# A hybrid backbone on one core: the gate matmuls of the recurrence branch interleaved with the next projection in another ratio, the last round filled with the first tile of the branch's gate projection, and its weights loaded one tile ahead

## The chip, the cores and the metric

One core of one Trainium2 chip. The metric is the device time of one execution in microseconds (us). Before the change three runs gave 1374.14, 1374.28 and 1376.15 us (median 1374.28).

## The reference

The program is a two-layer backbone over 1024 latent tokens of width 1024, with 256 context tokens. Layer 0 has two branches side by side. Branch A is a gated convolution (31 taps along the sequence, layer norm, SiLU). Branch B, which the change touches, is a gated linear recurrence in both directions:

```python
z = h @ p["w_in"]
va, vg, ga, xb, gb = jnp.split(z, [W_CONV, 2 * W_CONV, 3 * W_CONV, 3 * W_CONV + W_LRU], axis=-1)
y_a = conformer_conv(va, vg, p) * jax.nn.silu(ga)
y_b, hT = rglru_branch(xb, p, h0, True)
y_b = y_b * jax.nn.silu(gb)
return jnp.concatenate([y_a, y_b], axis=-1) @ p["w_out"], hT
```

In `rglru_branch` `xb` goes through a short convolution (4 taps) to `u`; two small matrices for each head and direction give the gates r and i (sigmoids); then a = exp(-8 r softplus(-lam)), the input is sqrt(1 - a^2) i u, and h = a h + input is scanned forwards and backwards, first over the context, then over the latent tokens. Layer 1 is a pooling mixer with two large projections; a final norm ends the program.

## The kernel before

Channels lie on the 128 partitions, tokens along the free dimension; the 1024 channels are 8 tiles (`KT` = 8). Every fp32 product is split into three matmuls of rounded parts: hi x hi, hi x lo, lo x hi (`mm3_steps`, L126 to L128, one step for each of the 8 tiles that are summed). A weight tile comes by DMA to `wr_*`, ScalarE (ACT) casts the high part `wh_*` (L95), GpSimd (POOL) subtracts for the low part `wl_*` (L96). `wr`, `wh` and `wl` have two buffers each (`wpool`), so a weight's cast waits until the matmuls of the weight before the last one are done. Results of 512 columns go to PSUM banks of the pool `pm` (4 of them, used in turn); `wide` tiles of 1024 columns lie in `pc`.

The branches of layer 0 start in a loop of 8 rounds, one for each channel tile j:

- the short convolution makes `uc` from the projections `xbc` (256 context columns) and `xb` (1024 latent columns): one ACT row (L531) and three VectorE (DVE) rows (L534) each; `uh` and `ul` (L538, L571) are its two parts.
- `decays(j - 1)` works on ACT: tanh of the r gates of the round before, their exp, and the root (all L449).
- `vg` and `va` are projected (48 matmuls each); ACT takes sigmoid(vg) as `sg` (L552), behind the root; DVE multiplies to `u` (L564), which also frees `va`'s two PSUM banks.
- `recurrence(j - 1)`: POOL multiplies (L463, L465), DVE forms the input (L468) and scans each direction over 256 (L475) and over 1024 (L477) columns; the sum of both (L480) is stored to DRAM (`yb_raw`).
- the gates of round j: 12 banks, of 256, 512 and 512 columns for each of the four gate tiles, three matmuls each (L508 to L510), ACT's sigmoid behind each (L511). Their steps are written interleaved with the 24 steps of the next round's `xb` projection (8 for the context, 16 for the latent columns), two after each bank, by `weave`.

In the last round there is no next `xb`: the `va` steps are interleaved with the gates instead. Behind the loop, the gate projection `gb` of branch B is made tile by tile (ACT's SiLU L726, DVE's product L727), then its output projection `wob`, while DVE works on the 31 taps of branch A's convolution (L746, 240 rows of about 1000 columns), which it takes up wherever it has nothing more urgent, from the first round on.

The written order isn't the order of issue. A scheduler orders the rows of each engine by priority and by its own estimate of when their inputs are ready; the order is fixed when the program is built, and each engine then works its queue in that order. `issue_after` and `high_priority` bind or move single rows. So a change in the written order moves rows on all engines.

Of the kernel before, what the change touches and what calls it, by code (L numbers as in the profile page):

```python
# [11 lines left out]
AF = mybir.ActivationFunctionType  # L12
# [3 lines left out]
P = 128  # L16
# [4 lines left out]
KT = D // P  # L21
# [34 lines left out]
def body(ctx, tc, xT, ctxT, cc, ccol, modT, modW, win, gw, wout, wu, grp, wg, wo1, small, edge, ident, outT):  # L56
# [30 lines left out]
    def psum(name):  # L87
        return pm.tile([P, H], F32, tag="mm", name=name)
# [341 lines left out]
    with ExitStack() as actx:  # L430
# [83 lines left out]

        def weave(some, others, n):
            for _ in some:
                for _ in range(n):
                    next(others, None)
            for _ in others:
                pass  # L520

        state = None
# [3 lines left out]
        for j in range(KT):  # L526
# [38 lines left out]

            gws = wload(gw[j], f"gw{j}", nc.gpsimd, n=4 * P) if last else None
            with ExitStack() as octx:
                if not last:
                    weave((), value_steps(), 1)
                    octx.enter_context(tc.issue_after(taken[0].ins))  # L570
                nc.vector.tensor_tensor(out=ul, in0=uc, in1=uh.bitcast(F32), op=sub)  # L571
            if last:
                weave(gate_steps(j, gws, (uh, ul), gates), value_steps(), 1)
            if j == 0:
# [4 lines left out]
            if state is not None:  # L579
                recurrence(j - 1, *state, roots)  # L580
            if not last:
                xb, steps = project_xb(j + 1)
                gws = wload(gw[j], f"gw{j}", nc.gpsimd, n=4 * P)
                weave(gate_steps(j, gws, (uh, ul), gates), steps, 2)
            state = uc, gates
        recurrence(KT - 1, *state, decays(KT - 1, state[1])[0])

# [127 lines left out]

    bh, bl = [], []
    for j in range(KT):
        w = wload(win[4 * KT + j], f"gb{j}", nc.gpsimd)
        th, tl = d2tile(f"ybh{j}", F32R), d2tile(f"ybl{j}", F32R)
        for h in range(2):  # L720
            ps = psum(f"gb{j}_{h}")
            mm3(ps, w, (hh, hl), HALF[h])
            y = vtile(f"yr{j}_{h}")
            nc.sync.dma_start(y, yb_raw[j][:, HALF[h]])
            sgt = ttile(f"sb{j}_{h}")
            nc.scalar.activation(sgt, ps, AF.Silu)  # L726
            nc.vector.tensor_tensor(out=y, in0=y, in1=sgt, op=mult)  # L727
            split(y, th[:, HALF[h]], tl[:, HALF[h]], nc.gpsimd)
        bh.append(th)
        bl.append(tl)  # L730
# [701 lines left out]
```

## Time and profile before

| | |
|---|---|
| median of 3 runs | 1374.28 us |
| profiled execution | 1381.07 us, its span 1379.3 us |
| PE (matmul) busy | 1295.9 us, 94% of the span |
| DVE busy | 1205.1 us, 87% |
| ACT busy | 632.7 us, 46% |
| POOL busy | 363.3 us, 26% |
| granted TensorE clock, mean | 0.974 |

The rounds lie between about 93 and 476 us of the span, `gb` up to 570, `wob` up to about 672. In rows of the profile a line is engine, line of the program, operation, output and inputs; "idle before" names what ended the engine's wait. A row of a timeline gives start and duration in us; consecutive rows overlap by a little, so what a row costs its engine is read from start to start.

### The profile page before, as it was taken

Reading aid. Unit: us, or ns where it says so; the run is one execution under the profiler, and the core shown is the slowest. Engines: PE = TensorE matmul, PEld = TensorE weight load, DVE = VectorE, ACT = ScalarE, POOL = GpSimd, SP = SyncE. Lnnn points to the kernel's source line nnn. Section 1 sums busy time; section 2 is a strip of 40 time slices with the busy share of each in tenths; the row PEclk is TensorE's granted clock in tenths of the full one; section 3 lists DMA queues with packets and bytes.
Section 4 is the critical chain, followed back from the end, with each engine's and each line's share of the span. In section 5 each row is a group of like instructions: output and inputs, shape, how many; then the busy total and the mean of one; then the engine's idle time right before and its main releaser. Section 6 shows DMA issues by size and latency. Waiting matters only on the chain.

```text
span 1379.3 us, 15637 instructions
## 1 busy us (share of the span) xinstructions
PE 1295.9 (94%) x5664; PEld 1048.2 (76%) x5664; DVE 1205.1 (87%) x1587; ACT 632.7 (46%) x906; POOL 363.3 (26%) x182
## 2 busy tenths in 40 slices
PE   7889989898999799999998999999999999999896
PEld 4468868787777587787887887788888888778685
DVE  7998999999999999998778865999999987876775
ACT  6353644674465542304533544754334344634442
POOL 5173534743473555523320004000000000000002
PEclk9899999999999899999999999999999999999997
DMA  9753011111112113343353646424243334758623
GB/s 354 280 180 119 25 59 54 53 40 61 54 35 72 46 46 130 110 151 135 103 185 122 221 154 205 138 93 151 100 145 123 115 115 132 265 190 275 206 107 123
DMA packets 82866, 181.79 MB, mean 132 GB/s; under 512 B 7778, under 2 KB 27618, under 8 KB 82788
## 3 DMA queue, kind: packets, MB, share of 16 engines
q1 hardware_dynamic: 74340, 176.60, 37.8%
q10 hardware_dynamic: 8448, 4.20, 1.0%
q8 instruction: 44, 0.72, 0.2%
q14 instruction: 34, 0.28, 0.1%
HBM read 136.72 MB, written 44.04 MB: 131 GB/s over the span
## 4 chain that ended last, share of the span: by engine, by line
PE 36%; DVE 10%; DMA 7%; issue 2%; ACT 2%; POOL 1%; POOLq 0%; SPq 0%; DVEq 0%; ACTq 0%
PE ga L127 2%; PE ga L128 2%; PE ga L126 2%; PE wob L127 2%; PE wob L128 2%; PE wob L126 2%; DMA wr_g<-wg 1%; DVE ws L986 1%; DMA yr_t<-y_t 1%; DMA wr_v<-wfold 1%; PE qb_g L666 1%; DVE wq_g L96 1%; PE qb_g L669 1%; PE qb_g L668 1%; DVE wq_wo L96 1%
## 5 line engine op out<-in xcount | busy, mean ns | idle before, releaser
L746 DVE SCALAR_TENSOR_TENSOR conv<-u,sm,conv 128x1013 f32<-128x1013 f32 (+14 forms) x232 | 291.2, 1272 | 6.6 <-ACT conv L738 3.8
L1252 POOL TENSOR_TENSOR o<-x,rr 128x256 f32<-128x256 f32 (+1 forms) x9 | 8.0, 923 | 462.9 <-ACT rr L1240 460.0
L511 ACT ACTIVATE g<-g,sm 128x512 f32<-128x512 f32 (+1 forms) x96 | 58.8, 617 | 110.5 <-PE g L510 108.3
L96 POOL TENSOR_TENSOR wl_wu<-wr_wu,wh_wu 128x1024 fp32r<-128x1024 f32 x16 | 39.4, 2470 | 153.9 <-ACT wh_wu L95 147.7
L463 POOL TENSOR_TENSOR g<-g,uc 128x1280 f32<-128x1280 f32 x16 | 47.5, 2967 | 107.9 <-ACT g L511 65.1
L249 PE MATMUL fold<-gh,wh_wu 128*128 128x512 f32 x128 | 53.0, 416 | 5.7 <-ACT wh_wu L95 5.7
L250 PE MATMUL fold<-gl,wh_wu 128*128 128x512 f32 x128 | 52.4, 409 | 3.2 <-DVE gl L96 3.2
L128 PE MATMUL gb<-h0h,wl_gb 128*128 128x512 f32 x128 | 50.7, 398 | 4.8 <-POOL wl_gb L96 4.8
L126 PE MATMUL vg<-h0h,wh_vg 128*128 128x512 f32 x128 | 52.3, 408 | 2.7 <-ACT g L511 2.1
L251 PE MATMUL fold<-gh,wl_wu 128*128 128x512 f32 x128 | 50.7, 405 | 2.3 <-POOL wl_wu L96 2.3
L128 PE MATMUL xb<-h0h,wl_xb 128*128 128x512 f32 x128 | 50.2, 392 | 2.0 <-POOL wl_xb L96 2.0
L127 PE MATMUL wob<-ybl,wh_wob 128*128 128x512 f32 x128 | 50.5, 395 | 1.2 <-POOL ybl L96 1.2
L465 POOL TENSOR_TENSOR g<-g,th 128x1280 f32<-128x1280 f32 x16 | 46.9, 2948 | 16.8 <-ACT th L449 16.8
L127 PE MATMUL vg<-h0l,wh_vg 128*128 128x512 f32 x128 | 51.2, 400 | 0.0
L126 PE MATMUL gb<-h0h,wh_gb 128*128 128x512 f32 x128 | 50.6, 395 | 0.1
L126 PE MATMUL va<-h0h,wh_va 128*128 128x512 f32 x128 | 50.6, 395 | 0.0
L127 PE MATMUL va<-h0l,wh_va 128*128 128x512 f32 x128 | 50.6, 395 | 0.0
L508 PE MATMUL g<-uh,wh_gw 128*128 128x512 f32 (+1 forms) x96 | 36.3, 379 | 15.1 <-ACT wh_gw L95 6.4
L126 PE MATMUL wob<-ybh,wh_wob 128*128 128x512 f32 x128 | 50.6, 396 | 0.0
L128 PE MATMUL wob<-ybh,wl_wob 128*128 128x512 f32 x128 | 49.9, 391 | 0.7 <-POOL wl_wob L96 0.7
L128 PE MATMUL va<-h0h,wl_va 128*128 128x512 f32 x128 | 50.4, 395 | 0.0
L127 PE MATMUL gb<-h0l,wh_gb 128*128 128x512 f32 x128 | 50.4, 393 | 0.0
(548 smaller groups left out, 4301.1 us busy)
## 6 DMA issues: line engine op xcount, KB each, us to landing
mod<-modT SPq DMA_DIRECT2D x28, 512.0 KB, 5.5
wr_wu<-wu SPq DMA_DIRECT2D x16, 512.0 KB, 3.9
x_part<-xp SPq DMA_DIRECT2D x32, 256.0 KB, 2.4
mod<-modT SPq DMA_DIRECT2D x32, 256.0 KB, 3.3
wr_v<-wfold SPq DMA_DIRECT2D x16, 512.0 KB, 3.7
wr_g<-wg SPq DMA_DIRECT2D x16, 512.0 KB, 5.4
wr_wo<-wo SPq DMA_DIRECT2D x16, 512.0 KB, 4.2
yr_t<-y_t SPq DMA_DIRECT2D x16, 512.0 KB, 6.3
```

Of the source, the lines that this page charges most:

```text
L96: eng.tensor_tensor(out=lo, in0=src, in1=hi.bitcast(F32), op=sub))
L126: nc.tensor.matmul(ps, hi[:, kc], xh[k][:, cols], start=(k == 0), stop=False)
L127: nc.tensor.matmul(ps, hi[:, kc], xl[k][:, cols], start=False, stop=False)
L128: nc.tensor.matmul(ps, lo[:, kc], xh[k][:, cols], start=False, stop=(k == ks - 1))
L249: nc.tensor.matmul(ps, wh[:, kc], gh[i], start=(i == 0), stop=False)
L250: nc.tensor.matmul(ps, wh[:, kc], gl[i], start=False, stop=False)
L251: nc.tensor.matmul(ps, wl[:, kc], gh[i], start=False, stop=(i == 3))
L463: nc.gpsimd.tensor_tensor(out=ius[d], in0=ius[d], in1=uc, op=mult)
L465: nc.gpsimd.tensor_tensor(out=ius[d], in0=ius[d], in1=roots[d], op=mult)
L508: nc.tensor.matmul(ps[:, :n], gwh[:, kc], uh[:, a : a + n], start=True, stop=False)
L511: nc.scalar.activation(t[:, a : a + n], ps[:, :n], AF.Sigmoid, bias=col(ob + d * KT + j))
L746: nc.vector.scalar_tensor_tensor(out=(us[j] if k == 30 else acp)[:, a:b], in0=us[j][:, a + o : b + o], scalar=col(O_CONVW + 31 * j + k), i ...
```

## The change

`weave` now takes `lead` steps of the projection alone first (8, the context part, in the rounds; 4 in the last), then one bank of gates and one step in turn, then what is left. The last round is now written like the others: the values first, then the recurrence of the round before, then the gates with a projection beside them, which is the latent `gb` projection of tile 0 (`project_gate`, into a wide tile). Its SiLU `sb0` is taken before the last recurrence, and the weights of the other `gb` tiles are loaded one tile ahead.

```diff
--- before.py
+++ after.py
@@ -512,12 +512,19 @@
                         yield
 
 
-        def weave(some, others, n):
+        def weave(some, others, lead):
+            for _ in range(lead):
+                next(others)
             for _ in some:
-                for _ in range(n):
-                    next(others, None)
+                next(others)
             for _ in others:
                 pass
+
+
+        def project_gate():
+            w = wload(win[4 * KT], "gb0", nc.gpsimd)
+            ps = wide("gb0", 1)
+            return ps, (x for h in range(2) for x in mm3_steps(ps[:, HALF[h]], w, (hh, hl), HALF[h]))
 
         state = None
         xb, steps = project_xb(0)
@@ -563,14 +570,10 @@
                     with tc.high_priority(offset=EVAC):
                         taken.append(nc.vector.tensor_tensor(out=u[:, HALF[h]], in0=ps, in1=sg[h], op=mult))
 
-            gws = wload(gw[j], f"gw{j}", nc.gpsimd, n=4 * P) if last else None
-            with ExitStack() as octx:
-                if not last:
-                    weave((), value_steps(), 1)
-                    octx.enter_context(tc.issue_after(taken[0].ins))
+            for _ in value_steps():
+                pass
+            with tc.issue_after(taken[0].ins):
                 nc.vector.tensor_tensor(out=ul, in0=uc, in1=uh.bitcast(F32), op=sub)
-            if last:
-                weave(gate_steps(j, gws, (uh, ul), gates), value_steps(), 1)
             if j == 0:
                 for m in range(2 * KT, 3 * KT):
                     raw = ltile(f"mod0_{m}")[:, :D]
@@ -578,11 +581,16 @@
                     mod_tile(m0, 0, m, raw, (cL,), raw)
             if state is not None:
                 recurrence(j - 1, *state, roots)
-            if not last:
+            if last:
+                gb0, steps = project_gate()
+            else:
                 xb, steps = project_xb(j + 1)
-                gws = wload(gw[j], f"gw{j}", nc.gpsimd, n=4 * P)
-                weave(gate_steps(j, gws, (uh, ul), gates), steps, 2)
+            gws = wload(gw[j], f"gw{j}", nc.gpsimd, n=4 * P)
+            weave(gate_steps(j, gws, (uh, ul), gates), steps, 4 if last else KT)
             state = uc, gates
+        sb0 = [ttile(f"sb0_{h}") for h in range(2)]
+        for h in range(2):
+            nc.scalar.activation(sb0[h], gb0[:, HALF[h]], AF.Silu)
         recurrence(KT - 1, *state, decays(KT - 1, state[1])[0])
 
     cpool.release()
@@ -714,16 +722,22 @@
 
 
     bh, bl = [], []
+    w_next = wload(win[4 * KT + 1], "gb1", nc.gpsimd)
     for j in range(KT):
-        w = wload(win[4 * KT + j], f"gb{j}", nc.gpsimd)
+        w = w_next
+        if 0 < j < KT - 1:
+            w_next = wload(win[4 * KT + j + 1], f"gb{j + 1}", nc.gpsimd)
         th, tl = d2tile(f"ybh{j}", F32R), d2tile(f"ybl{j}", F32R)
         for h in range(2):
-            ps = psum(f"gb{j}_{h}")
-            mm3(ps, w, (hh, hl), HALF[h])
+            if j == 0:
+                sgt = sb0[h]
+            else:
+                ps = psum(f"gb{j}_{h}")
+                mm3(ps, w, (hh, hl), HALF[h])
+                sgt = ttile(f"sb{j}_{h}")
+                nc.scalar.activation(sgt, ps, AF.Silu)
             y = vtile(f"yr{j}_{h}")
             nc.sync.dma_start(y, yb_raw[j][:, HALF[h]])
-            sgt = ttile(f"sb{j}_{h}")
-            nc.scalar.activation(sgt, ps, AF.Silu)
             nc.vector.tensor_tensor(out=y, in0=y, in1=sgt, op=mult)
             split(y, th[:, HALF[h]], tl[:, HALF[h]], nc.gpsimd)
         bh.append(th)
```

What it moves on the engines is seen at three places. The first is PE at the end of round 3, from the last matmul of `xb4` (before) or the last gate bank but one (now) up to the first `vg4`; names are tiles, `g3_1_1_768` is the bank of gate tile (direction 1, gate i) that begins at column 768. Before:

```order
L128 MATMUL xb4_1976<-h0h_7_649,wl_xb4_1972 128x512
L508 MATMUL g3_1_1_0_2086<-uh3_1826,wh_gw3_1979 128x256
L509 MATMUL g3_1_1_0_2086<-ul3_1827,wh_gw3_1979 128x256
L510 MATMUL g3_1_1_0_2086<-uh3_1826,wl_gw3_1980 128x256
L508 MATMUL g3_1_1_256_2097<-uh3_1826,wh_gw3_1979 128x512
L509 MATMUL g3_1_1_256_2097<-ul3_1827,wh_gw3_1979 128x512
L510 MATMUL g3_1_1_256_2097<-uh3_1826,wl_gw3_1980 128x512
L508 MATMUL g3_1_1_768_2108<-uh3_1826,wh_gw3_1979 128x512
L509 MATMUL g3_1_1_768_2108<-ul3_1827,wh_gw3_1979 128x512
L510 MATMUL g3_1_1_768_2108<-uh3_1826,wl_gw3_1980 128x512
L126 MATMUL vg4_0_2145<-h0h_0_585,wh_vg4_2141 128x512
```

Now:

```order
L510 MATMUL g3_1_1_256_2091<-uh3_1826,wl_gw3_1980 128x512
L128 MATMUL xb4_1976<-h0h_5_637,wl_xb4_1972 128x512
L126 MATMUL xb4_1976<-h0h_6_643,wh_xb4_1971 128x512
L127 MATMUL xb4_1976<-h0l_6_644,wh_xb4_1971 128x512
L128 MATMUL xb4_1976<-h0h_6_643,wl_xb4_1972 128x512
L126 MATMUL xb4_1976<-h0h_7_649,wh_xb4_1971 128x512
L127 MATMUL xb4_1976<-h0l_7_650,wh_xb4_1971 128x512
L128 MATMUL xb4_1976<-h0h_7_649,wl_xb4_1972 128x512
L508 MATMUL g3_1_1_768_2099<-uh3_1826,wh_gw3_1979 128x512
L509 MATMUL g3_1_1_768_2099<-ul3_1827,wh_gw3_1979 128x512
L510 MATMUL g3_1_1_768_2099<-uh3_1826,wl_gw3_1980 128x512
L126 MATMUL vg4_0_2145<-h0h_0_585,wh_vg4_2141 128x512
```

Seven matmuls of `xb4`, its end, now stand ahead of the round's last gate bank, where three banks stood together behind the end of `xb4`. At the round's begin, the 24 context matmuls `xbc4` now stand ahead of the first gate bank, where 21 of `xb4` stood.

The second place is ACT at the same time: sigmoids of the last gates (L511), tanh, exp and root of the decays (L449; `cneg` marks an exp, `tiny` a root), casts of the next weights. ACT_TABLE_LOAD is a load of ACT's function tables. Before:

```order
L449 ACTIVATE th3_0_2131<-g3_0_0_1983,chalf_127 128x1280
L449 ACTIVATE th3_1_2133<-g3_1_0_2051,chalf_127 128x1280
L511 ACTIVATE g3_1_1_2085<-g3_1_1_256_2097,sm_115 128x512
L95 CAST wh_va4_2201<-wr_va4_2199 128x1024
L511 ACTIVATE g3_1_1_2085<-g3_1_1_768_2108,sm_115 128x512
L449 ACT_TABLE_LOAD
L449 ACTIVATE g3_0_0_1983<-g3_0_0_1983,cneg_128 128x1280
L449 ACTIVATE g3_1_0_2051<-g3_1_0_2051,cneg_128 128x1280
L449 ACT_TABLE_LOAD
L449 ACTIVATE th3_0_2131<-th3_0_2131,tiny_125 128x1280
```

Now:

```order
L511 ACTIVATE g3_1_1_2082<-g3_1_1_256_2091,sm_115 128x512
L95 CAST wh_vg4_2141<-wr_vg4_2139 128x1024
L449 ACT_TABLE_LOAD
L449 ACTIVATE g3_0_0_2007<-g3_0_0_2007,cneg_128 128x1280
L538 ACTIVATE uc4_2119<-xb4_1976,sm_115 128x1024
L95 CAST wh_va4_2201<-wr_va4_2199 128x1024
L511 ACT_TABLE_LOAD
L511 ACTIVATE g3_1_1_2082<-g3_1_1_768_2099,sm_115 128x512
L449 ACT_TABLE_LOAD
L449 ACTIVATE g3_1_0_2057<-g3_1_0_2057,cneg_128 128x1280
L449 ACT_TABLE_LOAD
L449 ACTIVATE th3_0_2131<-th3_0_2131,tiny_125 128x1280
```

One exp now stands ahead of the last sigmoid, and four table loads stand between the second tanh and the first root, where there were two. The whole queue of ACT has 47 table loads, 33 before.

The third is DVE in round 2, in the recurrence of round 1, from its second input row up to the second half of `u2`; `conv1` rows are taps of branch A. Before:

```order
L468 SCALAR_TENSOR_TENSOR g1_1_1_1481<-g1_1_0_1447,g1_1_1_1481 128x1280
L564 TENSOR_TENSOR u2_1601<-va2_0_1602,sg2_0_1566 128x512
L571 TENSOR_TENSOR ul2_1525<-uc2_1515,uh2_1524 128x1280
L746 SCALAR_TENSOR_TENSOR conv1_3892<-u1_1299,sm_115,conv1_3892 128x1020
L477 SCALAR_TENSOR_TENSOR g1_0_1_1413<-g1_0_0_1379,g1_0_1_1413 128x1024
L475 SCALAR_TENSOR_TENSOR g1_1_1_1481<-g1_1_0_1447,g1_1_1_1481 128x256
L746 SCALAR_TENSOR_TENSOR conv1_3892<-u1_1299,sm_115,conv1_3892 128x1021
L564 TENSOR_TENSOR u2_1601<-va2_1_1628,sg2_1_1593 128x512
```

Now:

```order
L468 SCALAR_TENSOR_TENSOR g1_1_1_1478<-g1_1_0_1453,g1_1_1_1478 128x1280
L760 SCALAR_TENSOR_TENSOR conv1_3891<-u1_1299,sm_115,conv1_3891 128x1022
L477 SCALAR_TENSOR_TENSOR g1_0_1_1428<-g1_0_0_1403,g1_0_1_1428 128x1024
L475 SCALAR_TENSOR_TENSOR g1_1_1_1478<-g1_1_0_1453,g1_1_1_1478 128x256
L760 SCALAR_TENSOR_TENSOR conv1_3891<-u1_1299,sm_115,conv1_3891 128x1021
L477 SCALAR_TENSOR_TENSOR g1_1_1_1478<-g1_1_0_1453,g1_1_1_1478 128x1024
L760 SCALAR_TENSOR_TENSOR conv1_3891<-u1_1299,sm_115,conv1_3891 128x1020
L571 TENSOR_TENSOR u2_1601<-va2_0_1602,sg2_0_1566 128x512
L576 TENSOR_TENSOR ul2_1525<-uc2_1515,uh2_1524 128x1280
L480 TENSOR_TENSOR g1_0_1_1428<-g1_0_1_1428,g1_1_1_1478 128x1024
L760 SCALAR_TENSOR_TENSOR conv1_3891<-u1_1299,sm_115,conv1_3891 128x1019
L571 TENSOR_TENSOR u2_1601<-va2_1_1628,sg2_1_1593 128x512
```

Both long scans and the sum of both directions now stand ahead of the second half of `u2`, where one of the scans and the sum came behind it.

## The prediction

> **What bounds the kernel now.** I read the windows first, one to each round of the recurrence branch (a round begins where PE begins the `xb` projection for the next channel tile), then the two stages behind, then the rest. The columns are PE, PEld, DVE, ACT and POOL busy time with instruction counts, granted clock, DMA share, GB/s.
>
> ```profile
> 128.85:171.76 42.91, 42.78 (x206) 35.74 (x204) 37.84 (x31) 27.14 (x31) 21.48 (x8) 1.00 0.11 31
> 171.76:223.41 51.65, 46.76 (x205) 37.67 (x204) 48.43 (x40) 26.95 (x31) 21.80 (x8) 0.93 0.16 56
> 223.41:266.33 42.92, 42.79 (x205) 35.73 (x204) 42.53 (x36) 27.04 (x31) 22.18 (x9) 1.00 0.14 44
> 266.33:314.77 48.44, 44.91 (x205) 36.91 (x204) 48.08 (x38) 25.93 (x30) 26.88 (x10) 0.96 0.14 49
> 314.77:362.12 47.35, 43.75 (x205) 35.60 (x204) 45.43 (x38) 26.96 (x31) 24.41 (x10) 1.00 0.16 50
> 362.12:409.07 46.95, 44.56 (x205) 37.15 (x204) 44.76 (x37) 27.05 (x31) 22.59 (x10) 0.96 0.15 51
> 409.07:476.36 67.29, 55.27 (x241) 44.53 (x240) 65.05 (x51) 33.89 (x44) 27.13 (x10) 0.90 0.16 51
> 476.36:570.50 94.14, 89.36 (x385) 73.22 (x385) 92.52 (x77) 38.16 (x48) 54.45 (x29) 0.98 0.29 95
> 570.50:592.29 21.79, 19.94 (x85) 15.52 (x84) 21.79 (x22) 4.85 (x7) 9.86 (x6) 1.00 0.40 123
> 592.29:1379.30 787.01, 756.87 (x3303) 617.95 (x3302) 646.19 (x1052) 334.70 (x538) 70.28 (x45) 0.98 0.46 155
> ```
>
> A round without a stall takes 42.9 us, the others 47 to 52, with DVE busy nearly throughout. The last round takes 67, and `gb` 94.1 for 384 wide matmuls, which at 0.227 us each (below) are 87.2. Behind 592 PE leads to the end, so what PE loses before 592 is lost for good. The waits of PE between 128 and 592 say on what:
>
> ```profile
> PE g L509 <- DVE ul L571: 6.7, 3, 3.0
> PE g L508 <- ACT wh_gw L95: 6.4, 1, 6.4
> PE g L508 <- DVE u L564: 6.2, 3, 2.3
> ```
>
> In the rounds it is `u` and `ul`, which stand in DVE's queue behind the recurrence of the round before. So the rounds are a loop: gates (PE), sigmoid, tanh, exp, sqrt (ACT), the multiplication by the root (POOL), the recurrence and then `u` (DVE), and the third bank of the next gates, which reuses the PSUM bank that `u` frees. One turn is read from these rows of PE: a start after a wait for `u`, the next `vg`, the next such start.
>
> ```profile
> 323.89 0.50 PE L508 MATMUL g<-uh,wh_gw 128*128 128x512 f32 x1 [1.72 <-DVE u L564]
> 339.23 0.50 PE L126 MATMUL vg<-h0h,wh_vg 128*128 128x512 f32 x1 [0.55 <-ACT g L511]
> 371.79 0.62 PE L508 MATMUL g<-uh,wh_gw 128*128 128x512 f32 x1 [2.27 <-DVE u L564]
> ```
>
> The turn is 47.9 us: 15.3 of PE to `vg`, then 15.8 to the recurrence's first row on DVE,
>
> ```profile
> 354.99 4.24 DVE L468 SCALAR_TENSOR_TENSOR g<-g,g 128x1280 f32<-128x1280 f32 x1 [0.32 <-POOL g L465]
> ```
>
> and 16.8 from there to the `u` that frees the bank. The end of that stretch, with the scans and a convolution tap (L746) ahead of `u`:
>
> ```profile
> 367.05 2.34 DVE L477 TENSOR_TENSOR_SCAN g<-g,g 128x1024 f32<-128x1024 f32 x1
> 369.31 0.66 DVE L475 TENSOR_TENSOR_SCAN g<-g,g 128x256 f32<-128x256 f32 x1
> 369.89 1.25 DVE L746 SCALAR_TENSOR_TENSOR conv<-u,sm,conv 128x1022 f32<-128x1022 f32 x1
> 371.06 0.68 DVE L564 TENSOR_TENSOR u<-va,sg 128x512 f32<-128x512 f32 x1
> ```
>
> The second long scan and the sum of both directions came behind that `u`; the sum:
>
> ```profile
> 375.09 1.22 DVE L480 TENSOR_TENSOR g<-g,g 128x1024 f32<-128x1024 f32 x1
> ```
>
> **The change, part by part.** No arithmetic is added; the matmuls are the same in number. What counts is the order.
>
> *PE.* Starts of 512-wide matmuls lie 0.227 us apart (these two are eleven apart), of 256-wide ones 0.12 (the second pair):
>
> ```profile
> 314.77 0.39 PE L126 MATMUL xb<-h0h,wh_xb 128*128 128x512 f32 x1
> ...
> 317.27 0.39 PE L128 MATMUL xb<-h0h,wl_xb 128*128 128x512 f32 x1
> ```
>
> ```profile
> 108.85 0.28 PE L126 MATMUL xbc<-cth,wh_xb 128*128 128x256 f32 x1
> 108.97 0.28 PE L127 MATMUL xbc<-ctl,wh_xb 128*128 128x256 f32 x1
> ```
>
> Behind the third gate bank the old order has 48 wide and 21 narrow matmuls up to `vg` (13.4 us), the new one 64 and 10 (15.7), since the cheap context part now stands ahead of the wait and seven `xb` matmuls stand before the last gate. The measured 15.3 holds 1.2 us of waits, so 0.8 is slow clock after the stall; I keep that 0.8.
>
> *ACT.* The rows from a round's last gates to the root, of before:
>
> ```profile
> 243.26 1.20 ACT L531 ACTIVATE uc<-xb,sm 128x1024 f32<-128x1024 f32 x1
> 244.35 0.47 ACT L511 ACTIVATE g<-g,sm 128x256 f32<-128x256 f32 x1
> 244.70 2.62 ACT L449 ACTIVATE th<-g,chalf 128x1280 f32<-128x1280 f32 x2
> 247.21 0.68 ACT L511 ACTIVATE g<-g,sm 128x512 f32<-128x512 f32 x1
> 247.78 1.05 ACT L95 CAST wh_va<-wr_va 128x1024 fp32r<-128x1024 f32 x1
> 248.72 0.70 ACT L511 ACTIVATE g<-g,sm 128x512 f32<-128x512 f32 x1
> 249.44 1.28 ACT L449 ACT_TABLE_LOAD   x1
> 250.73 2.62 ACT L449 ACTIVATE g<-g,cneg 128x1280 f32<-128x1280 f32 x2
> 253.36 1.28 ACT L449 ACT_TABLE_LOAD   x1
> 254.66 2.62 ACT L449 ACTIVATE th<-th,tiny 128x1280 f32<-128x1280 f32 x2
> 256.16 5.89 POOL L465 TENSOR_TENSOR g<-g,th 128x1280 f32<-128x1280 f32 x2 [1.91 <-ACT th L449]
> ```
>
> In the new order the last gate comes out of PE so late that the first exp stands ahead of its sigmoid: load, exp, load, sigmoid, load, exp, load, root. The order has 47 table loads for 33: two more in five of the seven `vg` rounds (of the recurrences 0, 1, 3, 4, 6), four in the last. Summed by starts, from the gate before it on: 0.57 + 0.35 + 2.51 (two tanh) + 0.57 + 0.94 (`wh_vg`) + 1.29 + 1.31 + 1.09 + 0.94 + 1.29 + 0.58 + 1.29 + 1.31 + 1.29 + 1.31 = 16.7, and 3.1 for POOL's first product and the handover. That gate ends 51 wide and 7 narrow matmuls behind the third bank: 12.4 + 0.8. So third bank to recurrence is 33.0 us where the exps are split, 30.4 where not; it was 31.1.
>
> The Trainium skill, page "ScalarE: Activation LUTs", section "What ACT_TABLE_LOAD costs", gives about 1.28 us for the load and 1.38 more for a drain at every switch of tables. The trace agrees on the load only: the exp starts 1.29 us after the load did. By the page's sum each split would cost 2.8 us more.
>
> *DVE.* The new order puts the second 1024 scan (2.26 by starts) ahead of `u`, in the recurrences 0, 1, 2 also the sum (1.14, its 1.22 less the overlap of 0.08 that its neighbours show) and two more taps (1.17 each). So 16.8 becomes 22.5 three times, 19.0 for 3 and 6, 20.2 for 4 (scan, sum), 16.8 for 5.
>
> *The wait at `vg`.* Its weights reuse the buffer of `xb`'s, free only when PE is 0.7 us from `vg`. By the sum above the cast `wh_vg` ends 1.6 us after PE is ready for it, behind a load and an exp (recurrences 1 and 4) 4.2, and POOL's rest of the weights follows. Queued behind are `vg` and `va` on PE, and for those waits `u`. I cost it at nothing: 96 matmuls (21.8) and the way to the third bank (20 to 24 wide-matmul times, about 5) bring PE there some 43 us into the turn, and `u` comes at 47 to 55. That cover is 4 us in the shortest turn and 9 in most; where it is gone, up to 5 us a round are open.
>
> *Last round and `gb`.* `gb0` replaces the values as filler, and weights come a tile ahead: the wait of 6.4 and the 6.9 lost in `gb` go. Behind the third bank stand 49 wide and 10 narrow matmuls (12.3 + 0.8), then seven tiles of 48 at 0.227 = 76.3. Next to be late would be `sb3`, behind the recurrence's `yr1` in DVE's queue; by sums of the same rows it is about 2 us early. In the first 83 matmuls of `wob` (21.8 us for 19.1) I take the 2.7 us as gone too.
>
> *The sum.* Round 0 has no recurrence to wait for, so the first loop starts here:
>
> ```profile
> 149.56 0.39 PE L126 MATMUL vg<-h0h,wh_vg 128*128 128x512 f32 x1
> ```
>
> Plus 16.5 (16.7 + 3.1, less the 3.3 us of matmuls behind that gate) and 22.5: the first `u` frees its bank at 188.6. Then six turns: 55.5, 52.9, 52.0, 53.2, 47.2, 52.0 (312.8): 501.4. Plus 13.1 and 76.3: `wob` begins at 590.8, for 570.5, which is 20.3 late, less 2.7: **17.6 us slower**. The profiled execution took 1381.07 us with a span of 1379.3; the median of the runs is 6.8 below it, and I add the difference to the median: 1392.
>
> The bounds: an order in one queue gives no time back, so downwards there is only DVE without any wait. In order DVE has 13 more taps ahead of `u7` (164 for 151), 15.2 us at 1.17; one sum fewer, 1.1. Its idle time between 128.85 and 476.36 is 347.5 less 332.1 = 15.4.
>
> ```profile
> 479.02 0.68 DVE L564 TENSOR_TENSOR u<-va,sg 128x512 f32<-128x512 f32 x1
> ```
>
> With no wait at all `u7` ends at 479.7 + 15.2 - 1.1 - 15.4 = 478.4 for 501.4: 1369. That excludes the waits that I summed, so I take the sum. Upwards: the uncovered `vg` wait in three rounds, 1392 + 13 = 1405.
>
> **The rivals.** *Rounds as before, end gained (faster).* If DVE reaches the recurrence no later than now, the rounds keep their 47 to 48, and the end loses its stalls: 409.07 to 592.29 is 183.2 us, the matmuls in it are 635 wide and 36 narrow (148.5), two rounds' stalls of 5 remain: 158.5, 24.7 less, 1350. For it: half of PE's longest waits lie there. Against: it needs the table loads and scans off the loop, and the order has them on it; the 24.7 are used up when the eight turns grow by about 3 us each, and I sum 4 in the mean. *Waits absorbed (about the same).* DVE fills its waits with taps that must be done anyway; near 1372. Against: the taps of each turn stand ahead of or between the recurrence in fixed order. *The changed order isn't the one that is written.* PE takes 20 `xb` matmuls in a row between gates, not three; that is in the sum already. *Dearer switches.* If a switch of tables held ACT for twice its row of 1.28, the five splits of two would add 12.9: 1405; in the rows above the next activation follows at once. (The drain that the Trainium skill's page names would come to about that.)
>
> **How the numbers follow.** Forecast 0.80; faster end 0.08; absorbed 0.07; dearer switches or an open `vg` wait 0.05. The range 1377 to 1405 leaves out the first rival and the lower half of the second. A measurement of this kernel can tell about 0.2% (2.7 us) from no change. Faster by over 0.2% is the first rival and a part of the absorbed case: 0.09; within: 0.06; slower: 0.85.
>
> **What would show it.** Right: turns of 52 to 56 us from `u` to `u`, PE waiting for DVE `u` or `ul` by 4 to 8 us in rounds 1 to 6, 47 loads, a pair of loads around one sigmoid, `gb` without a stall, `wob` begun near 591. Wrong: turns of 48, waits named `wh_vg` or `wl_vg` in their place, or `gb` still stalled.

## The result and the profile after

The changed kernel takes 1422.78 us (median of 4 executions, 1420.16 to 1427.11), the kernel before beside it 1374.21 (4 executions, 1373.93 to 1376.15): a ratio of 1.0353, 95% interval 1.0321 to 1.0386, 48.6 us slower. The forecast was 1392, with a range of 1377 to 1405. The direction and the loop behind it were right, the size was not: 31 us are missing.

The profiled execution took 1420.45 us with a span of 1418.7, 39.4 more than the span profiled before. Windows of the changed kernel, one to each round and then the last round up to `gb1`, the rest of `gb`, and all that is behind; the columns are those of the prediction's first view (busy time of PE, PEld, DVE, ACT, POOL, then granted clock):

```profile
128.84:176.34 47.50, 44.41 (x206) 36.68 (x204) 40.30 (x33) 29.66 (x33) 21.45 (x8) 0.96 0.14 39
176.34:236.28 59.94, 48.58 (x206) 39.49 (x204) 55.54 (x45) 29.57 (x33) 21.55 (x8) 0.89 0.13 40
236.28:289.00 52.72, 46.27 (x206) 37.91 (x204) 49.23 (x41) 27.15 (x31) 25.59 (x10) 0.94 0.15 45
289.00:342.87 53.87, 46.55 (x205) 38.08 (x204) 46.14 (x40) 29.60 (x33) 22.71 (x10) 0.94 0.13 44
342.87:400.08 57.21, 48.51 (x206) 39.56 (x204) 54.84 (x44) 28.81 (x32) 20.26 (x8) 0.88 0.12 42
400.08:445.18 45.10, 43.07 (x206) 35.68 (x204) 44.13 (x37) 26.63 (x31) 24.99 (x10) 1.00 0.13 42
445.18:524.08 78.90, 65.98 (x290) 53.48 (x288) 73.89 (x61) 40.40 (x49) 30.96 (x13) 0.94 0.17 59
524.08:608.82 84.74, 80.58 (x337) 65.07 (x337) 75.76 (x59) 39.30 (x49) 45.50 (x25) 0.96 0.28 89
608.82:1418.70 809.88, 776.18 (x3387) 633.37 (x3385) 661.12 (x1061) 339.59 (x545) 81.91 (x51) 0.98 0.46 154
```

No round of 42.9 us is left, and the granted clock, 0.93 to 1.00 in the first six rounds of before, is 0.88 and 0.89 in the two longest. The `gb` window holds 336 wide matmuls for 384, since `gb0` stands in the last round: 84.74 us for 94.14 looks like a gain, but 48 matmuls at 0.227 are 10.9, so it is a loss of 1.5. The last window is 1.1 us longer than the two last of before together, 808.8. PE's waits in the changed kernel up to `wob`:

```profile
PE g L509 <- DVE ul L576: 21.6, 6, 6.3
PE vg L126 <- ACT wh_vg L95: 16.6, 6, 4.3
PE vg L128 <- POOL wl_vg L96: 3.8, 3, 1.3
PE gb L126 <- ACT g L511: 2.9, 1, 2.9
PE gb L128 <- POOL wl_gb L96: 2.6, 3, 1.0
...
PE gb L126 <- ACT sb L738: 1.6, 1, 1.6
```

The turn of recurrence 1, followed as the prediction followed one of before. The first `u` frees its PSUM bank at 188.7 (forecast 188.6). ScalarE between there and the root, with the pair of loads around one sigmoid that the order showed:

```profile
206.20 0.67 ACT L511 ACTIVATE g<-g,sm 128x512 f32<-128x512 f32 x1
206.89 1.28 ACT L449 ACT_TABLE_LOAD   x1
208.18 1.36 ACT L449 ACTIVATE g<-g,cneg 128x1280 f32<-128x1280 f32 x1
...
212.54 1.28 ACT L511 ACT_TABLE_LOAD   x1
213.83 0.69 ACT L511 ACTIVATE g<-g,sm 128x512 f32<-128x512 f32 x1
214.54 1.28 ACT L449 ACT_TABLE_LOAD   x1
215.84 1.36 ACT L449 ACTIVATE g<-g,cneg 128x1280 f32<-128x1280 f32 x1
```

and VectorE from the recurrence's first row to the `u` behind it:

```profile
223.00 4.22 DVE L468 SCALAR_TENSOR_TENSOR g<-g,g 128x1280 f32<-128x1280 f32 x1 [1.50 <-POOL g L465]
...
236.54 2.34 DVE L477 TENSOR_TENSOR_SCAN g<-g,g 128x1024 f32<-128x1024 f32 x1
238.81 1.25 DVE L760 SCALAR_TENSOR_TENSOR conv<-u,sm,conv 128x1020 f32<-128x1020 f32 x1
239.97 0.68 DVE L571 TENSOR_TENSOR u<-va,sg 128x512 f32<-128x512 f32 x1
240.57 1.48 DVE L576 TENSOR_TENSOR ul<-uc,uh 128x1280 fp32r<-128x1280 f32 x1
241.97 1.21 DVE L480 TENSOR_TENSOR g<-g,g 128x1024 f32<-128x1024 f32 x1
...
244.30 0.68 DVE L571 TENSOR_TENSOR u<-va,sg 128x512 f32<-128x512 f32 x1
```

From the bank to the recurrence 34.3 us (forecast 33.0), from there to the end of the second `u` at 244.98 22.0 (forecast 22.5): a turn of 56.3, forecast 55.5. What PE does behind such a stall is seen in its starts there:

```profile
185.82 0.58 PE L509 MATMUL g<-ul,wh_gw 128*128 128x256 f32 x1 [6.33 <-DVE ul L576]
186.20 0.63 PE L126 MATMUL xb<-h0h,wh_xb 128*128 128x512 f32 x1
186.63 0.63 PE L127 MATMUL xb<-h0l,wh_xb 128*128 128x512 f32 x1
```

Wide starts lie 0.425 us apart for 0.227. Summed over all pairs of 512-wide starts between 0.3 and 0.6 us apart, with no wait between them, from 128 us to `wob`, this costs 25.3 us, and 11.8 in the kernel before. The Trainium skill, page "TensorE: Matmul & The Clock Gate", section "The HAM clock gate", gives half rate (426.7 ns for 512 columns) after an idle window of about 3.4 us; the trace agrees on the rate, and differs on the window, since a stall of 2.68 us ahead of 242.11 was also followed by 3.4 us at that pace.

### The profile page after: what moved, and what is told of

Its sections match the earlier page's. It is cut to its first block, busy times and chain, and to the rows that moved or that the text cites. A ratio compares the mean times of both kernels' runs of the same rounds, so it can differ in the third digit from the quotient of the medians.

```text
span 1418.7 us, 15659 instructions
## 1 busy us (share of the span) xinstructions
PE 1309.1 (92%) x5664; PEld 1057.4 (75%) x5664; DVE 1213.5 (86%) x1587; ACT 650.7 (46%) x920; POOL 357.3 (25%) x182
## 4 chain that ended last, share of the span: by engine, by line
PE 46%; DVE 26%; ACT 9%; DMA 9%; issue 5%; POOL 4%; SPq 0%; POOLq 0%; ACTq 0%; DVEq 0%
DVE g L468 3%; DVE conv L760 3%; PE xb L127 2%; PE xb L126 2%; PE xb L128 2%; PE ga L127 2%; PE ga L126 2%; PE ga L128 2%; PE wob L127 2%; PE wob L128 2%; PE wob L126 2%; DVE ws L1000 2%; DVE g L477 2%; DMA wr_g<-wg 2%; ACT L449 1%
## 5 line engine op out<-in xcount | busy, mean ns | idle before, releaser
L760 DVE SCALAR_TENSOR_TENSOR conv<-u,sm,conv 128x1010 f32<-128x1010 f32 (+14 forms) x232 | 295.3, 1275 | 17.6 <-ACT conv L752 13.3
L511 ACT ACTIVATE g<-g,sm 128x512 f32<-128x512 f32 (+1 forms) x96 | 56.2, 615 | 102.0 <-PE g L510 101.0
L96 POOL TENSOR_TENSOR wl_wu<-wr_wu,wh_wu 128x1024 fp32r<-128x1024 f32 x16 | 39.4, 2469 | 152.9 <-ACT wh_wu L95 147.8
L126 PE MATMUL vg<-h0h,wh_vg 128*128 128x512 f32 x128 | 54.0, 422 | 16.8 <-ACT wh_vg L95 16.6
L468 DVE SCALAR_TENSOR_TENSOR g<-g,g 128x1280 f32<-128x1280 f32 x16 | 46.2, 2887 | 16.1 <-POOL g L465 16.1
L509 PE MATMUL g<-ul,wh_gw 128*128 128x512 f32 (+1 forms) x96 | 36.7, 382 | 21.6 <-DVE ul L576 21.6
L128 PE MATMUL vg<-h0h,wl_vg 128*128 128x512 f32 x128 | 52.9, 421 | 3.8 <-POOL wl_vg L96 3.8
L127 PE MATMUL xb<-h0l,wh_xb 128*128 128x512 f32 x128 | 53.0, 414 | 0.0
L126 PE MATMUL xb<-h0h,wh_xb 128*128 128x512 f32 x128 | 52.8, 413 | 0.0
```

What stands on the lines that cost most here:

```text
L96: eng.tensor_tensor(out=lo, in0=src, in1=hi.bitcast(F32), op=sub))
L126: nc.tensor.matmul(ps, hi[:, kc], xh[k][:, cols], start=(k == 0), stop=False)
L127: nc.tensor.matmul(ps, hi[:, kc], xl[k][:, cols], start=False, stop=False)
L128: nc.tensor.matmul(ps, lo[:, kc], xh[k][:, cols], start=False, stop=(k == ks - 1))
L468: nc.vector.scalar_tensor_tensor(out=iu, in0=at, scalar=1.0, in1=iu, op0=add, op1=mult)
L511: nc.scalar.activation(t[:, a : a + n], ps[:, :n], AF.Sigmoid, bias=col(ob + d * KT + j))
```

## The experiments

Theory: the loss is made in the rounds, by gates that come out of PE late, and with them late sigmoids, split exps and a late recurrence. Rivals: the end (last round, `gb0`, weights ahead); the table loads alone; the scans ahead of `u` alone; VectorE's load.

In this table "rounds" runs from the second start of `vg` to the last, "end" from there to the first `wob`, "behind" from there to the first matmul of `qc_woa`, the point of PE's first longer wait in the stage after `ga` (`wq_woa` is its weights). Stage times are of one profiled execution each; that of e3 lay 9 us below its median. The same rounds took between 282.1 and 287.0 us in the six kernels that have them as before (before, e2, e8, e14, e15, e16), so a difference of a few us between two stage times decides nothing.

| kernel | median, us | ratio to before (95%) | rounds | end | behind |
|---|---|---|---|---|---|
| before | 1374 to 1377 | 1 | 287.0 | 134.0 | 185.8 |
| changed | 1422.8 | 1.0353 (1.0321 to 1.0386) | 322.3 | 135.0 | 188.0 |
| e1, rounds only | 1423.9 | 1.0341 (1.0312 to 1.0371) | 322.2 | 137.9 | 185.9 |
| e2, end only | 1380.1 | 1.0017 (1.0000 to 1.0034) | 282.1 | 132.1 | 188.0 |
| e3, exps behind | 1401.8 | 1.0159 (1.0118 to 1.0200) | 303.0 | 135.4 | 184.5 |
| e4, scan behind | 1426.4 | 1.0353 (1.0324 to 1.0382) | 324.7 | 137.3 | 185.8 |
| e5, lead 12 | 1382.6 | 1.0041 (1.0017 to 1.0066) | 284.4 | 134.8 | 189.1 |
| e6, lead 24 | 1380.1 | 1.0028 (1.0009 to 1.0046) | 287.2 | 131.6 | 187.6 |
| e8, e2 + Silu behind | 1382.7 | 1.0050 (1.0024 to 1.0076) | 285.0 | 132.5 | 193.8 |
| e9, e6 + Silu behind | 1388.6 | 1.0086 (1.0060 to 1.0111) | 288.6 | 133.7 | 192.6 |
| e10, e3 + e5 | 1387.4 | 1.0071 (1.0053 to 1.0089) | 287.7 | 135.5 | 187.4 |
| e14, e2 + early lo | 1382.3 | 1.0048 (1.0028 to 1.0069) | 286.9 | 133.2 | 189.3 |
| e15, e8 + early lo | 1382.2 | 1.0039 (1.0020 to 1.0059) | 284.9 | 133.4 | 190.3 |
| e16, before + early lo | 1373.2 | 0.9977 (0.9955 to 0.9998) | 284.9 | 133.4 | 184.7 |
| e17, e5 + early lo | 1385.7 | 1.0071 (1.0043 to 1.0098) | 285.5 | 131.3 | 195.1 |

### Which half: e1 and e2

The two halves of the change, each alone. e1 is the kernel before with this in rounds 0 to 6:

```
-                weave(gate_steps(j, gws, (uh, ul), gates), steps, 2)
+                for _ in range(KT):
+                    next(steps)
+                weave(gate_steps(j, gws, (uh, ul), gates), steps, 1)
```

> The new weave (eight projection steps alone, then a bank of gates and a step in turn) in rounds 0 to 6, with the last round and the gb loop of before. Theory A (the loss is made in the rounds): vg of the last round began 37.4 us later in the changed kernel (473.87 for 436.52), so this takes about 1374 + 35 = 1409, between 1400 and 1420. Rival B (a good part of the loss comes from the last round, from gb0 in it, or from weights that are fetched a tile ahead): under 1395.

e2 is the changed kernel with two steps behind each bank in rounds 0 to 6:

```
-            weave(gate_steps(j, gws, (uh, ul), gates), steps, 4 if last else KT)
+            if last:
+                weave(gate_steps(j, gws, (uh, ul), gates), steps, 4)
+            else:
+                for _ in gate_steps(j, gws, (uh, ul), gates):
+                    next(steps)
+                    next(steps)
```

> The other half alone: rounds 0 to 6 with two projection steps behind each bank of gates as before, the last round with gb0 as its filler and the gb loop with weights a tile ahead as changed. Theory A: the rounds keep turns of 47 to 48 us and the stalls of 6.4 us ahead of the last gates and 6.9 us in gb go, so 1374 - 13 = 1361, between 1352 and 1370: faster than both. Rival B (the end is itself a loss, since gb stalled in the changed kernel as well, 84.7 us for the 76.3 that I summed): 1374 or more. Third possibility (the end only has a gain where PE arrives late): 1374 within 3.

e1 took 1423.9, the whole loss and 4 us more than theory A's range. e2 took 1380.1, where A had 1361: the end gains nothing, as both its rivals had it. The stalls that were counted as 13 us did go (`wh_gw` of the last round, `wl_gb`), but others stand in their place, 1.8 us for `u` and these. PE's longest waits in e2 from the last `vg` to `wob`:

```profile
PE gb L126 <- ACT g L511: 6.9, 1, 6.9
PE gb L126 <- ACT sb L743: 2.6, 1, 2.6
```

### What in the rounds: e3, e4, e5, e6, e10

e3 chains the tanh and exps behind the round's last gate sigmoid, as the chain of `decays` already does among themselves:

```
-            rs, roots, last = gates[0::2], [], None
+            rs, roots, last = gates[0::2], [], gate_end[0]
...
-                        nc.scalar.activation(t[:, a : a + n], ps[:, :n], AF.Sigmoid, ...
+                        gate_end[0] = nc.scalar.activation(t[:, a : a + n], ps[:, :n], AF.Sigmoid, ...
```

> The changed kernel with the tanh and exps of a round held behind the round's last gate sigmoid in ScalarE's queue, so that no sigmoid stands between two exps: 37 table loads for 47 (in the rounds with a split, 1.29 + 1.31 us of loads and the exp between go from ahead of the last sigmoid). The scheduler then also moves the second scan and the sum of three of the seven recurrences behind u. Theory A1 (table loads on the loop are the larger part): five turns shorter by 2.6 to 5 us each, 1422.8 - 13 to 25 = 1398 to 1410. Rival A2 (the loads are paid beside other waits, and the scans ahead of u or the weights of vg are what counts): 1413 to 1423.

e4 holds the scan of the second direction behind `ul`:

```
+                    if d and behind is not None:
+                        octx.enter_context(tc.issue_after(behind.ins))
                     nc.vector.tensor_tensor_scan(out=iu[:, ctx_], ...
...
-                recurrence(j - 1, *state, roots)
+                recurrence(j - 1, *state, roots, ul_done)
```

> The changed kernel with the long scan of the second direction (and with it the sum) held behind ul on VectorE, as the order of before had it; ScalarE's table loads stay (49 for 47). Theory A2 (scan and sum ahead of u and ul are the larger part): each of six turns shorter by the scan of 2.3 us, in three by the sum of 1.1 as well: 6 x 2.3 + 3 x 1.1 = 17 us, 1406, between 1400 and 1411. Rival A1 (the loop is set by the table loads, or by vg's weights that come late): 1415 to 1425.

e3 took 1401.8: 21 us of the loss, inside what A1 expected. The binding also moved scans behind `u`, as its expectation says, so the 21 us are not of the table loads alone. PE's wait for `wh_vg` fell from 16.6 us to 2.2, since the cast no longer stands among loads and exps; the wait for `ul` stayed, 23.3:

```profile
PE g L509 <- DVE ul L576: 23.3, 7, 4.8
...
PE vg L126 <- ACT wh_vg L95: 2.2, 6, 0.6
```

e4 took 1426.4 where A2 had 1406: holding the scans back, alone, gains no time. Its waits for `u` and `ul` fell to 20.4 us from 24.1, and those for `wh_vg` rose to 21.6 from 16.6.

e5 and e6 only change how many projection steps stand alone ahead of the gates. Both take `next(others, None)` in `weave`, so that an empty projection ends nothing; this line is e5's, e6 has 24 for 12:

```
-            weave(gate_steps(j, gws, (uh, ul), gates), steps, 4 if last else KT)
+            weave(gate_steps(j, gws, (uh, ul), gates), steps, 4 if last else 12)
```

> The changed kernel with twelve projection steps alone ahead of the gates for eight, so that the one-in-turn part uses up the projection and no step is left behind the last bank. Theory D (the turn is set by what PE does between the third bank and the last gates and vg, and by the table loads that follow from late gates): twelve wide matmuls less there, 2.7 us in each of six turns, and 39 table loads for 47, about two splits of 2.6 us or more: 1422.8 - 16 to 30 = 1393 to 1407. Rival C (any long run of projection ahead of the gates delays the third bank and loses): 1415 or more.

> The changed kernel with the whole projection (24 steps) ahead of the gates and nothing between the banks. Theory D: only 18 wide and 9 narrow matmuls are left between the third bank and vg, about 5 us for the 15 of the changed kernel, and 37 table loads for 47, so u comes in time, PE's waits for u and ul go, and the turn is set by VectorE's own queue (45 to 46 us of work a round) or PE's 42.9: 1352 to 1370, faster than before. Rival C (without filler between them the banks wait for ScalarE's sigmoids, and the longer run ahead delays the third bank): 1400 or more, with waits for PSUM banks (g, ScalarE) between the gates.

e5 took 1382.6, 40 us of the 45 to 49: more than theory D had. Four steps moved are 2.7 us a turn on PE, the rounds shrank by 37.9 us, 6.3 a turn. The rest is what comes with it. ScalarE in e5, where the gate is now there before the exps and they stay together:

```profile
208.08 0.70 ACT L511 ACTIVATE g<-g,sm 128x512 f32<-128x512 f32 x1
208.80 1.28 ACT L449 ACT_TABLE_LOAD   x1
210.09 2.62 ACT L449 ACTIVATE g<-g,cneg 128x1280 f32<-128x1280 f32 x2
```

and VectorE in e5, the first `u` and `ul` ahead of the second direction's scans:

```profile
219.58 3.20 DVE L468 SCALAR_TENSOR_TENSOR g<-g,g 128x1280 f32<-128x1280 f32 x1
...
230.61 0.66 DVE L571 TENSOR_TENSOR u<-va,sg 128x512 f32<-128x512 f32 x1
231.19 1.48 DVE L576 TENSOR_TENSOR ul<-uc,uh 128x1280 fp32r<-128x1280 f32 x1
...
234.97 2.34 DVE L477 TENSOR_TENSOR_SCAN g<-g,g 128x1024 f32<-128x1024 f32 x1
```

In that turn the recurrence needs 13.1 us to the end of `ul`, 19.1 in the changed kernel (223.00 to 242.05). e6 missed: 1380.1 for 1352 to 1370. Its waits for `ul` fell to 2.2 us, but the gates now waited for `uc` (10.4) and for PSUM banks (8.0, the wait that rival C named), and the context matmuls for `wl_xb` (6.0).

e10 puts e3's binding into e5.

> Both cures of the rounds: twelve projection steps ahead (e5) and the tanh and exps behind the last gate's sigmoid (e3). e3 alone left 24 us of the loss (1401.8), e5 alone 5 (1382.6), so the two overlap. Theory D1 (late gates make the splits; once PE is through by twelve matmuls earlier, nothing is left for the binding to gain): 1380 to 1385, as e5. Rival D2 (each takes its own part, so that the rest of e5's waits is the two splits that it still has): 1375 or less. Against e3 it shows what the twelve matmuls are worth by themselves: 17 to 22 us under D1.

1387.4: nothing is added, as D1 said (it had 1380 to 1385, and 17 to 22 less than e3; it was 14). So the table loads are no cause by themselves: binding them, with the scans that moved along, is worth 21 us where the gates are late, and nothing where they are not.

### VectorE's load or its order: e11, e12, e13

Each leaves out ten taps of the 31-tap convolution in all eight tiles:

```
-            if k != 15:
+            if k >= 10 and k != 15:
```

> The kernel before without the first ten taps of the 31-tap convolution in each of the eight channel tiles (80 instructions of VectorE of about 1.2 us left out, 96 us; the output is that of a shorter convolution). It is the base line for the next run. Theory F (VectorE's queue, nearly full ahead of wob, holds PE there): most of the 30 us that PE stands still between 128 and 592 us goes, 1340 to 1360. Rival G (PE's order, the weights and ScalarE hold it): 1368 to 1377.

> Rounds as before with the changed last round and gb loop (e2), with the same ten taps left out. Theory F (in e2 the stalls that the end saves come back because Silu tiles, gb's products and PSUM banks wait for VectorE, which stood behind taps): with a shorter queue the end gains what I summed, 6.4 + 6.9 us: 10 to 15 us less than e11. Rival G (the last round's waits are ScalarE's own order, a Silu pair and its two table loads among the gates, or the recurrence's length): within 4 us of e11.

> The changed kernel with the same ten taps left out. If the rounds' loss were VectorE's load, it would be gone: within 10 us of e11. By the loop (gates late on PE, two table loads more on ScalarE, all scans ahead of u and ul), only the two to four taps of a turn that stood among the scans go, 2.4 to 4.8 us in each of six turns: 1395 to 1410, 40 or more above e11.

e11 took 1383.9 (ratio 1.0050, 1.0031 to 1.0069), e12 1390.2 (1.0094, 1.0074 to 1.0115), e13 1440.8 (1.0457, 1.0437 to 1.0478). Theory F falls: VectorE was busy for 80 us less (1125.3 for 1205.1 in e11), and nothing is faster. The rivals' times missed too: e11 had 1368 to 1377, and e12, the end alone, was to stay within 4 us of e11 and is 6 slower. The loop's expectation for e13 held in the difference (57 us above e11, 40 or more expected) and missed in the time (1395 to 1410). With the taps gone the scheduler put everything else in another order: in e13 it stands with both scans and the sum ahead of `u` and `ul` in each turn. PE's waits in e13:

```profile
PE g L509 <- DVE ul L576: 31.2, 7, 5.7
PE vg L126 <- ACT wh_vg L95: 14.8, 7, 3.8
```

So a queue with less in it gives no time back. That the place in the queue decides instead fits e13, but how much of its extra loss is that order and how much the taps' absence was not told apart.

### Where the end's gain went: e8, e9, e14 to e17

The changed kernel at `gb1`: PE waits for a PSUM bank that a gate's sigmoid has to free, and ScalarE has that sigmoid behind a cast, a load, the two Silu of `gb0` and a load back.

```profile
518.58 1.05 ACT L95 CAST wh_gb<-wr_gb 128x1024 fp32r<-128x1024 f32 x1 [1.18 <-PE gb L127]
519.65 1.28 ACT L593 ACT_TABLE_LOAD   x1
520.94 1.08 ACT L593 ACTIVATE sb<-gb 128x512 f32<-128x512 f32 x2
522.04 1.28 ACT L511 ACT_TABLE_LOAD   x1
523.34 1.05 ACT L511 ACTIVATE g<-g,sm 128x512 f32<-128x512 f32 x2
```

```profile
524.08 0.50 PE L126 MATMUL gb<-h0h,wh_gb 128*128 128x512 f32 x1 [2.94 <-ACT g L511]
```

e8 is e2 with the pair behind the last gate (`gate_end[0]` is its sigmoid, kept as in e3), e9 the same in e6:

```
-        for h in range(2):
-            nc.scalar.activation(sb0[h], gb0[:, HALF[h]], AF.Silu)
+        with tc.issue_after(gate_end[0].ins):
+            for h in range(2):
+                nc.scalar.activation(sb0[h], gb0[:, HALF[h]], AF.Silu)
```

> Rounds as before and the end as changed (the run e2), with the two Silu of gb0 held behind the last gate's sigmoid. In e2 PE waited 6.9 us at gb1 for a PSUM bank, and ScalarE's queue had a convolution start that waited 4.2 us for VectorE, a cast, a table load, two Silu and a second load ahead of the sigmoid that frees it. Theory E1 (Silu and its two loads make that wait): 1.28 + 1.09 + 1.28 = 3.7 us go from the 6.9, and the time is 1380 - 3.7 = 1376. Rival E2 (the convolution start that waits makes it): the wait stays above 5 us and the time at 1380.

> The whole projection ahead of the gates (as in e6) and the two Silu of gb0 behind the last gate's sigmoid (as in e8). If both theories D and E1 hold, 3 to 4 us less than e6, 1350 to 1366; if only D holds, the same as e6; if neither holds, 1400 or more.

In e8 the wait fell from 6.9 to 3.1 us, by about the 3.7 that E1 counted, and the time didn't (1382.7): the wait for the Silu tiles of `gb3` grew from 2.6 to 4.7. e9 took 1388.6 and fitted none of its cases. PE's longest waits in e8 from the last `vg` to `wob`:

```profile
PE gb L126 <- ACT sb L744: 4.7, 1, 4.7
PE gb L126 <- ACT g L511: 3.1, 1, 3.1
```

That second wait hangs on the last recurrence. In e2 GpSimd's first `ybl` waits for the store of its sum, because the tile lies where the recurrence's tiles lay, and the next `yr`, Silu tiles and weights wait behind it. The kernel before has the same wait, 16.61 us at 520.86. In e2:

```profile
521.11 2.55 POOL L96 TENSOR_TENSOR ybl<-yr,ybh 128x512 fp32r<-128x512 f32 x2 [13.70 <-DMA yb_raw<-g]
```

That sum comes later in the new last round: 80.4 us behind the last `vg` before (436.52 to 516.87), 88.4 in the changed kernel (473.87 to 562.28), 86.4 in e2 (430.70 to 517.10). Before, the gates stood ahead of `va` in that round; now `va`, two more table loads and the Silu pair lie ahead of the root. e14 to e17 ("early lo" in the table) put the first two pairs of `yb` operands into memory that was free before:

```
-    d2pool = ctx.enter_context(tc.tile_pool(name="d2pool", bufs=16, reuse_waits="tile"))
+    d2a = ctx.enter_context(tc.tile_pool(name="d2a", bufs=4, reuse_waits="tile"))
+    d2b = ctx.enter_context(tc.tile_pool(name="d2b", bufs=12, reuse_waits="tile"))
...
```

> The run e2 (rounds as before, end as changed) with the tiles of the first two pairs ybh and ybl in memory that the recurrence's tiles never used, so that GpSimd's first ybl doesn't wait for the store of the last recurrence. Theory H (the last recurrence's end holds the gb loop through that wait: yr loads, Silu tiles, PSUM banks): the stall of 2.6 us at gb3 and what PE lost there in clock go, and wob no longer starts a fixed 46 us behind the last recurrence's sum: 3 to 6 us less than e2's 1380, 1374 to 1377. Rival I (the end is held by ScalarE and by PE's own order; that wait had cover): 1379 to 1382.

> The same in e8, where the Silu pair of gb0 is behind the last gate's sigmoid as well. Theory H: both stalls (3.1 us at gb1 with the pair moved, 4.7 at gb3) shrink to the first alone, 1380 - 8 = 1372, between 1368 and 1375. Rival I: 1380 to 1384, as e8.

> The kernel before with that wait taken away alone. In it gb stalled by 1.5 and 3.3 us for the rest of the weights (wl_gb), which stand behind ybl in GpSimd's queue. Theory H: the 3.3 us go and some clock with them, 3 to 5 us less than before. Rival I: within 2 us of before.

> The changed kernel with twelve steps ahead for eight (e5, 1382.6) and that wait taken away. Theory H: the stall of 4.9 us at gb3 goes, 1375 to 1378. Rival I: 1381 to 1384.

PE's waits for Silu tiles went in all of e14, e15 and e17, and no time with them (1382.3, 1382.2, 1385.7): rival I, in e17 2 us above its range. GpSimd's wait for the store did not go, it moved to the third pair's `ybl`, which still lies in the recurrence's memory (10.55, 9.72 and 10.53 us), so these runs don't show the end without it. In e15 the weights' second part, behind `ybl` in GpSimd's queue, took the place of the Silu tiles:

```profile
PE gb L128 <- POOL wl_gb L96: 6.6, 2, 3.4
```

In the kernel before (e16) GpSimd's wait for the store is gone, and the median is 3.2 us lower, about what theory H expected, with an interval that barely excludes no change; it is the one kernel here whose median lies below that of the kernel before. But the wait that was to go stayed, 4.2 us for 4.8, so where the 3.2 us come from isn't shown. PE's wait in e16:

```profile
PE gb L128 <- POOL wl_gb L96: 4.2, 3, 2.0
```

There is one more place, PE's first matmul of `qc_woa`, 184 to 195 us behind `wob`. In e2:

```profile
750.78 0.76 PE L679 MATMUL qc_woa<-ya_t1h,wq_woa 128*128 128x512 f32 x1 [4.48 <-ACT wq_woa L95]
```

It waits for weights that stand in VectorE's and ScalarE's queues there, 2.46 us both in the kernel before and in the changed one, 4.48 in e2, 6.84 in e5, 6.79 in e15. From the last `vg` to this point the kernel before takes 319.8 us, e2 320.1, the changed kernel 323.0, e5 323.9, e15 323.7. So in e2, e5 and e15 a longer wait here goes with no gain by this point; that it alone uses up what the end saved isn't shown, since these are differences of a few us between single executions.

## Why the prediction was right in direction and wrong in size

**The rounds as a loop: right, with another wait in it.** From one bank freed by `u` to the next the turns were 56.3, 54.3, 54.4, 53.7, 46.9 and 53.9 us (the second `u` of a round ends at 188.68, 244.97, 299.25, 353.62, 407.28, 454.18 and 508.09), forecast 55.5, 52.9, 52.0, 53.2, 47.2, 52.0. But PE seldom waited for that bank. In rounds 1 to 4 and 6 it waited earlier, for `ul` at the second matmul of the first bank (185.82, 242.11, 296.38, 349.65, 451.87), and came to the third bank 0.6 to 4.0 us after `u` had freed it. Counting from `u` gave nearly the right turns because `ul` was done only 2.4 to 4.6 us before that `u`; this much was luck. The split exps, the pair of loads around a sigmoid, the scans ahead of `u` stood where the order had them, and e1 shows that this half makes the whole loss.

**The slow clock: mis-sized.** "I keep that 0.8" held for a turn with one stall of 2 us. Now `ul` comes later still and `vg` waits too, and PE is slow behind both; ten wide starts at 0.425 us behind the first stall alone cost 2.0. The last `u` bank was taken at 508.15 for 501.4: 6.7 us, about 1.1 a turn. In the turn followed above PE, slow behind the stall, began the third bank at 191.08, 2.4 us after it was free, and had fewer matmuls behind it than summed, 11.5 us for 13.2. The other turns weren't taken apart, so that the clock makes all of the 6.7 isn't shown.

**The wait at `vg`: cover held but in one round, with a price.** It was 16.6 us for `wh_vg` and 3.8 for `wl_vg`, up to 4.3, in the two rounds where the prediction named 4.2, and `ul` was mostly later still: 2.7 to 4.2 us of wait for it were left in rounds 2 to 4 and 6. In round 5, behind a wait of 4.3 at `vg`, none was left; PE came to the gates 2.3 us after `ul` and then waited 1.9 for `wh_gw`. What the wait at `vg` cost by the clock, or by what it moved elsewhere, was not tried by itself.

**The last round and `gb`: the step that failed.** "The wait of 6.4 and the 6.9 lost in `gb` go", "seven tiles at 0.227 = 76.3". The wait of 6.4 went, of the 4.8 for `wl_gb` 2.6 stayed, and others came: from the last `u` bank to `gb1` 15.9 us for 13.1 (the 2.9 behind the Silu pair), and 84.7 for 76.3 in `gb` (2.6 for `wl_gb`, 1.6 for `sb`, the rest the clock behind them and smaller gaps). I had "`sb3` next late" early by 2 us; it hangs on a store that I hadn't counted, at the end of a recurrence that had become longer. Together 11.2 us; e2 shows that the end without the rounds' lateness gains nothing either.

**`wob`'s 2.7 taken as gone: wrong.** The first 84 matmuls of `wob` took 24.1 us, where 19.1 was summed and 21.8 measured before: PE waited 1.9 us for `ybh` and `ybl`, and ahead of these for the weights.

```profile
611.43 0.50 PE L128 MATMUL wob<-ybh,wl_wob 128*128 128x512 f32 x1 [2.00 <-POOL wl_wob L96]
```

From `wob` to the end the span was 1.1 us longer, not 2.7 shorter. "What PE loses before 592 is lost for good" held here: behind those 84 matmuls 785.8 us are left, 787.0 before. It doesn't hold for e5, whose `wob` begins only 1.1 us later than before and whose 84 matmuls take 19.0: behind them come 793.5 us, with the longer wait at `qc_woa` among them.

**The profile beside the median.** Of the miss of 30.8 us, 21.8 is in the spans (39.4 for 17.6): 6.7 + 2.8 + 8.4 + 3.8 = 21.7 (turns, up to `gb1`, `gb`, from `wob` on). The other 9 are chance: I took the span difference as that of the medians, but the profiled execution of before was 6.8 us above its median, and that of the changed kernel 2.3 below. Twenty-five later executions of the kernel before ran from 1372.5 to 1384.6, so 12 us of spread stand behind any single profile here; the range should have held that too.

**The rivals.** *Dearer switches*: no; 206.89 plus 1.28 is followed by the exp at 208.18. The Trainium skill's drain ("ScalarE: Activation LUTs", "What ACT_TABLE_LOAD costs") isn't seen here either. *Rounds as before, end gained*: e2 is that case, and it is not 1350. *Waits absorbed*: no.

What stays open: why the end gains nothing, that is, which wait would hold the end last if all that were found (Silu pair, `ybl`, `wl_gb`, `wq_woa`) were taken away at once, and how the loss of a turn divides between PE, loads and scans. e3, e4, e5 and e10 show that these don't add: the scheduler sorts the queues anew for each.

## What to carry to other kernels

In a loop over several in-order engines, one late product (here a gate, by 2.3 us of matmuls) can be paid on each engine that it passes: on PE, then by a split pair of table loads, then by scans that get ahead of what PE waits for, and once more by the clock behind the stall. The rows show each of these, not the share of each. Cure the first lateness (four steps more ahead of the gates brought back 40 us); binding a later member of the chain helps only as long as the first is late. Take a saved stall as a gain only after following each engine's queue to the next point where PE meets it: of 13 us "gone" at the end none arrived.

## What the runs showed of the hardware

PE ran at half pace (0.425 us a wide start) in thirteen stretches in the changed kernel up to `wob`, all behind waits, among them one behind waits of 1.58 and 0.55 us (572.43 and 573.72). It doesn't always begin with the first matmul: behind the wait that ended at 524.08 the next starts lie 0.23 to 0.33 us apart, and the slow stretch begins at 525.6. The granted clock (the third number from the end) shows why:

```profile
524.08:525.54 1.46, 1.46 (x6) 1.23 (x7) 1.43 (x2) 1.46 (x3) 0.00 (x0) 1.00 0.65 264
525.54:528.95 3.41, 3.41 (x9) 2.64 (x8) 1.92 (x3) 3.41 (x6) 0.59 (x1) 0.50 0.00 0
```

In this trace every stretch at clock 0.50 between 128 us and `wob` lasts 3.41 us (eight of them) or 6.83 (five), and all begin on one grid of 3.41 us, at 153.49, 184.21, 211.52, 242.24 and so on, whatever PE does at that moment. In the 3.41 us ahead of each, PE's rows show 1.7 to 3.4 us of idle time. So where a wait falls on the grid counts as well as its length: in the kernel before, whose grid meets 180.88 and 372.03, a wait of 2.20 us that ended at 181.36 was followed by clock 1.00, one of 2.27 that ended at 371.79 by 3.41 us at 0.50. Up to `wob` the clock stood at 0.50 for 61.4 us in the changed kernel, and for 30.7 in the kernel before.
